# An attention kernel for short sequences: no pairing copy of q and k rows, transposes in column halves, two load buffers of each

## Chip, cores, metric

One core of one Trainium2 chip. The metric is the device time of one execution in microseconds (us), as a median over repeated runs, and as a ratio. Ratios are the mean time of one kernel's fast runs over that of the other's fast runs of the same rounds, so they are not quite the ratio of the medians that are quoted. A run is called slow when it is over 1.5% above the fastest of its kernel; verdicts use the fast ones. The profile is of one execution; its span is that of the program on the core, 1.8 us under the time of the same execution.

## The reference

```python
batch, n_heads, seq, head_dim = 32, 12, 128, 64        # q, k, v: f32, randn * 0.1
scores = matmul(q, k^T) / sqrt(64)
attn   = exp(scores - max); attn = attn / (sum(attn) + 1e-8)
out    = matmul(attn, v)
```

384 heads of 128 x 64. Every input and the output is 12.58 MB in f32.

## The kernel before

Units of 8 heads, 48 in all. A "super" is four units: one slab of q, one of k and one group of v, 1 MiB of f32 each, turned into bf16 by the load (the page has 512.0 KB landed per load). GpSimd (POOL) issues all 36 loads and 40 of the 48 stores, in one queue. A unit takes one step; in a step TensorE transposes a quarter of the q and k slabs of a later super (half of one slab in each step), puts the rows of one v unit in order, computes the scores of the next unit and the values of the present one. VectorE copies the transposes out of PSUM (the tiles that end in `_ps`) and normalises; ScalarE does exp and copies v.

The parts that matter here, cut (cuts are marked by `# ...`):

```python
NQ, NVB, NVE, NP, NT, NA = 4, 2, 8, 4, 2, 4        # four buffers of q and of k, two of v
PERIOD, FIRST = 8, -8
TRIPS = NU // PERIOD + 1                           # NU = 48 units, 7 trips

def transposes(t):                                 # TensorE, 8 to a step
    x = pair[t_index[t] % NP]
    # ...
    for r in range(8):
        i = nc.tensor.transpose(p[:, :, r4, jj, :], x[:, r].rearrange("p a d -> p (a d)"), ident[:])

def pair_up(t):                                    # VectorE: rows of two half slabs side by side
    src = (q_b, k_b)[j][s % NQ][:].rearrange("p a (r d) -> p r a d", d=D)
    return nc.vector.tensor_copy(pair[t_index[t] % NP][:], src[:, 8 * b:8 * b + 8])

def pool_load(kind, x):
    # v: waits until TensorE has ordered group x - 2; q and k: until slab x - NQ has been paired
    # ...

# TensorE alone runs a loop; the other engines' programs are straight.
with nc.Fori(0, TRIPS, engines=..., head_slot={nc.tensor.engine: 128}):
    for skipped, always, some in places:           # eight steps, each with T, V, S, O
        run_waits("PE", always)
        with nc.tensor.If_ne(trip, skipped):       # the first or the last trip skips this part
            for o, w in some:
                run("PE", o, w)
```

Two things in this loop will matter. The program holds eight steps of code, and the first trip begins at step -8, of which three steps are empty: it jumps over their code, and over scores and values that are not due yet. And `head_slot` sets the place in TensorE's code at which the loop begins, here 128; runs below move it.

The softmax here doesn't subtract the row's maximum and nothing guards it: scores larger than these inputs give would overflow.

Of the kernel before, what the change touches and what calls it, by code (L numbers as in the profile page):

```python
# [10 lines left out]
def kernel(  # L11
# [7 lines left out]
    nc = tc.nc  # L19
    f32 = mybir.dt.float32  # L20
    bf16 = mybir.dt.bfloat16
    EXP = mybir.ActivationFunctionType.Exp

    B, H, S, D = q.shape
# [7 lines left out]
    NU = B * H // 8  # L32
# [25 lines left out]
    vgroups = [4] * (NU // 4)  # L58
# [13 lines left out]
    t_at, v_at = {}, {}  # L72
    for s, (R, f) in enumerate(supers):
        J = R // 4
        for x in range(J):
            j, b = divmod(x, J // 2)
            t_at.setdefault(f - J - 1 + x, []).append((s, j, b))
    for m in range(NU):
        v_at[m - 3] = [m]
    steps = range(min(t_at) - 2, NU + 1)  # L80

    NQ, NVB, NVE, NP, NT, NA = 4, 2, 8, 4, 2, 4



    MIXED, OWN, HELD = 24, 40, NU - 8
# [3 lines left out]
    def sb(name, shape, dtype):  # L90
        return ctx.enter_context(nc.sbuf_tensor(name, shape, dtype))
# [5 lines left out]
    ident = sb("ident", [128, 128], bf16)  # L97
    sel = {R: sb(f"sel{R}", [128, 8, 2, 32], bf16) for R in (16,)}
    q_b = [sb(f"q_b{i}", [128, 2, 16 * D], bf16) for i in range(NQ)]
    k_b = [sb(f"k_b{i}", [128, 2, 16 * D], bf16) for i in range(NQ)]  # L100
    v_b = [sb(f"v_b{i}", [128, 4, RV * D], bf16) for i in range(NVB)]
    v_e = [sb(f"v_e{i}", [128, 8, D + 1], bf16) for i in range(NVE)]
    pair = [sb(f"pair{i}", [128, 8, 2, D], bf16) for i in range(NP)]
    qkT = [sb(f"qkT{i}", [128, 2, 16, S], bf16) for i in range(NT)]
    attnT = [sb(f"attnT{i}", [128, 2, 4, S], bf16) for i in range(NA)]
    o_sb = [sb(f"o_sb{c}", [128, n * 2 * RO * D], f32) for c, n in enumerate(stores)]
# [16 lines left out]
    program = {e: [] for e in ("PE", "ACT", "DVE", "POOL", "SP")}  # L123
# [5 lines left out]
    def op(engine, key, emit, deps=(), marks=(), dma=()):  # L129
        o = Op()  # L130
        o.key, o.emit, o.deps, o.marks, o.dma = key, emit, deps, marks, dma
        assert key not in position, key
        position[key], engine_of[key] = len(program[engine]), engine
        program[engine].append(o)
# [34 lines left out]
    def transposes(t):  # L169

        s, j, b = t
        R = supers[s][0]
        x = pair[t_index[t] % NP]
        p = qk_ps[:].rearrange("p (h r j s) -> p h r j s", h=R, r=4, j=2)
        for r in range(8):
            jj, r4 = divmod(r, 4)
            i = nc.tensor.transpose(  # L177
                p[:, :, r4, jj, :], x[:, r].rearrange("p a d -> p (a d)"), ident[:])
        return i

    def order_v(m):
# [61 lines left out]
            in_=s_ps[u % 2][:].rearrange("p a (h r j s) -> p (a h r) s j", h=4, r=4, j=J),  # L243
            func=EXP, bias=0.0, scale=scale)

    def pair_up(t):

        s, j, b = t
        src = (q_b, k_b)[j][s % NQ][:].rearrange("p a (r d) -> p r a d", d=D)
        return nc.vector.tensor_copy(pair[t_index[t] % NP][:], src[:, 8 * b:8 * b + 8])  # L250

    def keep_qk(t):
        s, j, b = t
        R = supers[s][0]
        J = R // 4
        x = qkT[s % NT][:, j, :R, :]
        if J == 2:
            return nc.vector.tensor_copy(x.rearrange("p h x -> p (h x)"), qk_ps[:])
        return nc.vector.tensor_copy(  # L259
            x.rearrange("p h (r j s) -> p (h r) j s", r=4, j=J)[:, :, 2 * b:2 * b + 2, :].rearrange(  # L260
                "p x j s -> p x (j s)"),
            qk_ps[:].rearrange("p (x y) -> p x y", x=R * 4))
# [15 lines left out]
    t_order = [t for u in steps for t in t_at.get(u, [])]  # L278
    t_index = {t: i for i, t in enumerate(t_order)}
    t_step = {t: u for u in steps for t in t_at.get(u, [])}  # L280
    vstep_of = {m: u for u in v_at for m in v_at[u]}
    s_q = [tc.alloc_semaphore(f"s_q{i}") for i in range(NQ)]
    s_k = [tc.alloc_semaphore(f"s_k{i}") for i in range(NQ)]
# [7 lines left out]

    def pe_transposes(t):
        i = t_index[t]
        deps = [("P", t)] + ([("E", t_order[i - 1])] if i else [])
        op("PE", ("T", t), lambda: transposes(t), deps, ["pe_dve"])

    def pe_wait(kind, key):
        op("PE", (kind, None), None, [key])
# [18 lines left out]
    def v_landing(m):  # L317
        if m == NU or vplace[m][1]:
            return []
        g = vplace[m][0]  # L320
        return [(s_v[g % NVB], 16 * (g // NVB + 1))]
# [8 lines left out]
        deps = [("S", u)] + ([("Q", u - NA)] if u >= NA else [])  # L330
        op("ACT", ("X", u), lambda: exps(u), deps, ["act_pe"])

    def dve_pair(t):
        s, j, b = t
        deps = [("T", t_order[t_index[t] - NP])] if t_index[t] >= NP else []
        dma = [((s_q, s_k)[j][s % NQ], 16 * (s // NQ + 1))]
        op("DVE", ("P", t), lambda: pair_up(t), deps, ["dve_io"] if t_index[t] else ["dve_pe", "dve_io"], dma)

    def dve_keep(t):
        s = t[0]  # L340
        deps = [("T", t)]
        for x in range(s):
            if x % NT == s % NT:
                R, f = supers[x]
                deps.append(("S", f + R // 4 - 1))
        op("DVE", ("E", t), lambda: keep_qk(t), deps, ["dve_pe"])

    def dve_normalise(u):
        c, w, n, first = splace[u]
# [10 lines left out]
    def pieces(c):  # L360

        first = sum(stores[:c])
        return 2 if 1 < stores[c] < supers[of_unit[first]][0] // 4 else 1

    own = [c for c in range(len(stores)) if sum(stores[:c + 1]) <= OWN]

    def lane(c):

        return c % 4 + (4 if c in own else 0)

    def store(c):
        name = "POOL" if c in own else "SP"
        e = ENGINE[name]
        n = stores[c]
        first = sum(stores[:c])
        R, f = supers[of_unit[first]]
        J = R // 4

        def emit():
            dst = o_rows[:, 2 * f:2 * f + 2 * J, :].rearrange("p (a w) e -> p a w e", a=2)[  # L380
                :, :, first - f:first - f + n, :]
            src = o_sb[c][:].rearrange("p (a w e) -> p a w e", a=2, w=n)
            if pieces(c) == 1:
                e.dma_start(out=dst, in_=src).then_inc(s_o[lane(c)], 16)  # L384
            else:
                for a in range(2):
                    e.dma_start(out=dst[:, a], in_=src[:, a]).then_inc(s_o[lane(c)], 16)  # L387

        last = first + n - 1
        op(name, ("store", c), emit, [("N", last if c in own else max(last, HELD))])  # L390

    def pool_load(kind, x):
        deps = []
        if kind == "v":
            if x >= NVB:
                deps = [("V", sum(vgroups[:x - NVB + 1]) - 1)]
            n, first = vgroups[x], sum(vgroups[:x])
            op("POOL", ("load", kind, x), lambda: nc.gpsimd.dma_start(  # L398
                out=v_b[x % NVB][:, :n, :], in_=v_rows[:, first:first + n, :],
            ).then_inc(s_v[x % NVB], 16), deps)  # L400
            return
        R, f = supers[x]
        j = "qk".index(kind)
        rows, bufs, sm = ((q_rows, q_b, s_q), (k_rows, k_b, s_k))[j]
        if x >= NQ:
            deps = [("P", t) for t in t_order if t[0] == x - NQ and t[1] == j]
        n = f * 8 // R

        def emit():
            nc.gpsimd.dma_start(  # L410
                out=bufs[x % NQ][:], in_=rows[R][:, n:n + 2, :]).then_inc(sm[x % NQ], 16)

        op("POOL", ("load", kind, x), emit, deps)


    op("ACT", ("K", -1), lambda: nc.scalar.drain(), [], ["act_pe"], v_landing(0))
    at_step = {}
    for u in steps:
        start = len(program["PE"])
        for t in t_at.get(u, []):  # L420
            pe_transposes(t)
        if u == t_step[t_order[-1]] + 1:
            pe_wait("T", ("E", t_order[-1]))
        for m in v_at.get(u, []):
            pe_order_v(m)
            act_keep(m)
        if u - 1 == vstep_of[NU - 1]:
            pe_wait("V", ("K", NU - 1))
        if 0 <= u + 1 < NU:
            pe_scores(u + 1)  # L430
            act_exps(u + 1)
        if 0 <= u < NU:
            pe_values(u)
        if 0 <= u - 1:
            dve_normalise(u - 1)
        elif u == 0:
            op("DVE", ("M", -1), None, [], ["dve_pe"])
            op("DVE", ("N", -1), lambda: nc.vector.drain(), [], ["dve_pe"])
        for t in t_at.get(u, []):
            dve_keep(t)  # L440
        for t in t_at.get(u + 2, []):
            dve_pair(t)
        for o in program["PE"][start:]:
            at_step[o.key] = u

    loads = []
    for s in range(len(supers)):
        for j in range(2):
            loads.append((t_step[s, j, 0] - 2, "qk"[j], s))
    for g in range(len(vgroups)):  # L450
        m = sum(vgroups[:g])

        loads.append((vstep_of[m] - 1.5 + (2 if 2 <= g < len(vgroups) - 2 else 0), "v", g))
    loads.sort(key=lambda e: e[0])
    todo = list(range(len(stores)))
    for _, kind, x in loads:
# [3 lines left out]
    for c in todo:  # L460
        store(c)

    c = counts()
    seen = {e: {} for e in program}
    waited_dma = {e: {} for e in program}

    def waits_of(engine, o):
        out = []
# [133 lines left out]
```

## Time and profile before

| | before |
|---|---|
| time, median of 4 runs | 132.18 us (131.85 to 133.28) |
| span of the profiled run, which took 133.72 us | 131.9 us |
| read and written in HBM | 37.75 and 12.58 MB |
| TensorE, VectorE, ScalarE busy | 74, 69, 56% |
| last v group landed | 113.70 us |

The prediction below shows the lines for the bound (transfers), the gap in them and a step on the engines. What it leaves out are the groups that the change touches. Columns: line, engine, operation, output from inputs, shapes, count; then total busy time and mean of one in ns; then idle time of the engine before them.

```profile
L177 PE MATMUL qk_ps<-ident,pair 128*128 128x128 bf16 x384 | 32.2, 232 | 15.3 <-PEq L478 15.1
...
L177 PEld LDWEIGHTS qk_ps<-ident,pair 128*128 128x128 bf16 x384 | 24.2, 103 | 20.4 <-issue 17.9
...
L250 DVE COPY pair<-q_b 128x1024 bf16<-128x1024 bf16 x24 | 11.1, 460 | 6.3 <-DMA q_b<-in_q_dram 6.2
L250 DVE COPY pair<-k_b 128x1024 bf16<-128x1024 bf16 x24 | 10.2, 427 | 0.0
```

Eight transposes of 128 columns to a step, 384 in all, each with one load of 128 stationary columns (128x128 in the LDWEIGHTS row), and 48 pairing copies of 0.44 us on VectorE. One more part of the page also belongs here, and I passed over it: the table of DMA queues (packets, MB, share of the 16 engines' time).

```profile
q0 software_dynamic: 16064, 29.36, 101.3%
q1 hardware_dynamic: 2176, 2.10, 4.7%
q8 instruction: 4, 0.07, 0.2%
```

Queue 8 carries four packets, 0.07 MB, and the table calls its content instructions. That they are TensorE's I take from the experiments: in a_first5 TensorE goes on 2.3 to 2.4 us after the start of each of three such packets.

One thing about this profile was passed over as well: its execution took 133.72 us, longer than any of the four timed ones and 1.5 us over their median. It counts as fast, but it is not a typical run.

### The profile page before, as it was taken

The page shows a single profiled execution, that of the slowest core. Times are in us where ns is not written, and L with a number is a line of the kernel's source. Part 1 is how long each engine was busy: PE and PEld are TensorE (multiplying, and loading weights), DVE is VectorE, ACT ScalarE, POOL GpSimd, SP SyncE. Part 2 cuts the span into 40 slices and gives each one's busy share as a digit, 9 for nine tenths or more (in the row PEclk, how much of TensorE's full clock was granted, in tenths as well). Part 3 has the DMA queues.
Part 4 walks back from the last instruction along what each step waited for, and adds up shares of the span by engine and source line. Part 5 has one row for each costly group of instructions (what it writes and reads, how often), then busy time and mean ns, then how long its engine had stood idle before and what let it go on. Part 6 is the DMA issues. An engine that isn't in the chain of part 4 may idle for free. (4 is left out here: it accounts for less than half of the span.)

```text
span 131.9 us, 7079 instructions
## 1 busy us (share of the span) xinstructions
PE 97.0 (74%) x3072; PEld 68.9 (52%) x3072; DVE 90.8 (69%) x214; ACT 73.7 (56%) x97; POOL 55.5 (42%) x81
## 2 busy tenths in 40 slices
PE   0014989994989999869849839978669998877610
PEld 0013647672667677656627626656456766555410
DVE  1126366895588999969939848969826988875740
ACT  0000528845577778476367366498084868588700
POOL 5950005015008259194460391390680399930000
PEclk9999999999599999999999999999986999999955
DMA  2999999999999999999999999999999999999982
GB/s 15 164 206 210 208 208 213 209 207 212 204 213 165 167 222 237 209 327 251 208 318 259 209 279 217 212 353 220 212 348 225 211 342 270 400 380 368 319 289 82
DMA packets 18248, 31.56 MB, mean 239 GB/s; under 512 B 1344, under 2 KB 9536, under 8 KB 18240
## 3 DMA queue, kind: packets, MB, share of 16 engines
q0 software_dynamic: 16064, 29.36, 101.3%
q1 hardware_dynamic: 2176, 2.10, 4.7%
q8 instruction: 4, 0.07, 0.2%
q14 instruction: 4, 0.03, 0.1%
HBM read 37.75 MB, written 12.58 MB: 381 GB/s over the span
## 5 line engine op out<-in xcount | busy, mean ns | idle before, releaser
L241 ACT ACTIVATE attnT<-s_ps 128x1024 bf16<-128x1024 f32 x48 | 49.4, 1030 | 0.4 <-PE s_ps L217 0.4
L236 ACT CAST v_e<-v_ps 128x512 bf16<-128x512 f32 x48 | 28.2, 588 | 37.0 <-PE v_ps L191 19.1
L177 PE MATMUL qk_ps<-ident,pair 128*128 128x128 bf16 x384 | 32.2, 232 | 15.3 <-PEq L478 15.1
L191 PE MATMUL v_ps<-v_b,sel 128*32 128x256 bf16 x768 | 31.9, 289 | 11.3 <-PEq L478 11.2
L272 DVE TENSOR_TENSOR o_sb<-o_ps,recip 128x512 f32<-128x512 f32 (+1 forms) x53 | 34.0, 641 | 4.8
L259 DVE COPY qkT<-qk_ps 128x1024 bf16<-128x1024 bf16 x48 | 32.8, 684 | 5.3 <-PE qk_ps L177 4.3
L177 PEld LDWEIGHTS qk_ps<-ident,pair 128*128 128x128 bf16 x384 | 24.2, 103 | 20.4 <-issue 17.9
L398 POOL DMA_DIRECT2D v_b<-in_v_dram x12 | 9.5, 791 | 59.7 <-PE v_ps L191 59.7
L387 POOL DMA_DIRECT2D out_dram<-o_sb x38 | 27.2, 729 | 0.0
L191 PEld LDWEIGHTS v_ps<-v_b,sel 128*32 128x32 bf16 x768 | 16.9, 99 | 17.8 <-issue 13.6
L228 PE MATMUL o_ps<-v_e,attnT 128*32 128x65 bf16 x1536 | 22.6, 200 | 1.7 <-PEq L478 0.8
L269 DVE RECIPROCAL recip<-o_ps 128x8 f32<-128x8 f32 (+1 forms) x53 | 10.5, 198 | 16.8 <-PE o_ps L228 16.0
L228 PEld LDWEIGHTS o_ps<-v_e,attnT 128*32 128x32 bf16 x1536 | 16.7, 98 | 7.5 <-issue 3.8
L217 PE MATMUL s_ps<-qkT 64*128 64x128 bf16 x384 | 19.5, 222 | 0.7 <-PEq L478 0.6
L217 PEld LDWEIGHTS s_ps<-qkT 64*128 64x128 bf16 x384 | 11.1, 95 | 11.3 <-issue 11.3
L250 DVE COPY pair<-q_b 128x1024 bf16<-128x1024 bf16 x24 | 11.1, 460 | 6.3 <-DMA q_b<-in_q_dram 6.2
L250 DVE COPY pair<-k_b 128x1024 bf16<-128x1024 bf16 x24 | 10.2, 427 | 0.0
L410 POOL DMA_DIRECT2D q_b<-in_q_dram x12 | 9.0, 747 | 1.0 <-SPq L96 1.0
L236 ACT ACT_TABLE_LOAD x1 | 1.3, 1283 | 13.7 <-DMA v_b<-in_v_dram 13.7
L410 POOL DMA_DIRECT2D k_b<-in_k_dram x12 | 8.6, 721 | 0.0
L560 DVE COPY sel<-ident 128x128 bf16<-128x128 bf16 x2 | 0.4, 224 | 1.8 <-POOL ident L537 1.8
L384 POOL DMA_DIRECT2D out_dram<-o_sb x2 | 1.5, 734 | 0.0
(8 smaller groups left out, 1.4 us busy)
## 6 DMA issues: line engine op xcount, KB each, us to landing
out_dram<-o_sb POOLq DMA_DIRECT2D x40, 256.0 KB, 10.2
q_b<-in_q_dram POOLq DMA_DIRECT2D x12, 512.0 KB, 13.2
k_b<-in_k_dram POOLq DMA_DIRECT2D x12, 512.0 KB, 12.7
v_b<-in_v_dram POOLq DMA_DIRECT2D x12, 512.0 KB, 10.2
out_dram<-o_sb SPq DMA_DIRECT2D x8, 256.0 KB, 4.3
```

Source lines behind the costliest of these rows:

```text
L177: i = nc.tensor.transpose(p[:, :, r4, jj, :], x[:, r].rearrange("p a d -> p (a d)"), ident[:])
L191: x = nc.tensor.matmul(t[r4 * 32:(r4 + 1) * 32, i, :, :], lhsT=pick[:, w * nh + i, jv, :], rhs=v_b[g % NVB][:, :n, (4 * jv + r4) * D:(4 * ...
L217: i = nc.tensor.matmul(t[:, a, h, :], lhsT=x[p, 1, 4 * w + h, :], rhs=x[p, 0, 4 * w + h, :], start=True, stop=True)
L228: y = nc.tensor.matmul(t[h * SO:(h + 1) * SO, a, r * (D + 1):(r + 1) * (D + 1)], lhsT=x[:, a, h, r * SO:(r + 1) * SO], rhs=v_e[m % NVE][:, ...
L236: return nc.scalar.copy(v_e[m % NVE][:, :, :D], v_ps[:].rearrange("p (n e) -> p n e", e=D))
L241: return nc.scalar.activation(out=attnT[u % NA][:].rearrange("p a h (r s j) -> p (a h r) s j", r=4, j=J), in_=s_ps[u % 2][:].rearrange("p ...
L250: return nc.vector.tensor_copy(pair[t_index[t] % NP][:], src[:, 8 * b:8 * b + 8])
L259: return nc.vector.tensor_copy(x.rearrange("p h (r j s) -> p (h r) j s", r=4, j=J)[:, :, 2 * b:2 * b + 2, :].rearrange("p x j s -> p x (j ...
L269: nc.vector.reciprocal(r, o4[:, :, :, D]).then_inc(s_r, 1)
L272: return nc.vector.tensor_mul(o[:, :, w, :].rearrange("p a (r d) -> p a r d", d=D), o4[:, :, :, :D], r.unsqueeze(3).to_broadcast([128, o4. ...
L387: e.dma_start(out=dst[:, a], in_=src[:, a]).then_inc(s_o[lane(c)], 16)
L410: nc.gpsimd.dma_start(out=bufs[x % NQ][:], in_=rows[R][:, n:n + 2, :]).then_inc(sm[x % NQ], 16)
```

## The change

The intent: the pairing copy only brings two rows of 64 together so that one transpose fills 128 columns. TensorE can take either row from the landed tile and write it to its own half of the PSUM partitions (the changed kernel's page has 768 such transposes, with loads of 128x64), so VectorE loses 48 copies, and with the copies gone the number of q and k buffers falls from four to two (the loop's code names the buffers, and eight steps hold two supers). The core of the diff:

```diff
-    NQ, NVB, NVE, NP, NT, NA = 4, 2, 8, 4, 2, 4
+    NQ, NVB, NVE, NT, NA = 2, 2, 8, 2, 4
@@ transposes
-        x = pair[t_index[t] % NP]
+        x = (q_b, k_b)[j][s % NQ][:].rearrange("p a (r d) -> p r a d", d=D)[:, 8 * b:8 * b + 8]
         for r in range(8):
             jj, r4 = divmod(r, 4)
-            i = nc.tensor.transpose(
-                p[:, :, r4, jj, :], x[:, r].rearrange("p a d -> p (a d)"), ident[:])
+            for a in range(2):
+                i = nc.tensor.transpose(
+                    p[a * D:(a + 1) * D, :, r4, jj, :], x[:, r, a], ident[:])
@@ the landing of the next slab is now waited for ahead of the copy out of PSUM
-        op("DVE", ("E", t), lambda: keep_qk(t), deps, ["dve_pe"])
+        op("DVE", ("E", t), lambda: keep_qk(t), deps, ["dve_pe"], qk_landing(t_index[t] + 1))
@@ pool_load
-            deps = [("P", t) for t in t_order if t[0] == x - NQ and t[1] == j]
+            deps = [("T", t) for t in t_order if t[0] == x - NQ and t[1] == j]
@@ order of the loads
-            loads.append((t_step[s, j, 0] - 2, "qk"[j], s))
+            loads.append((t_step[s, j, 0], "qk"[j], s))
-        loads.append((vstep_of[m] - 1.5 + (2 if 2 <= g < len(vgroups) - 2 else 0), "v", g))
+        loads.append((vstep_of[m] + 0.5, "v", g))
```

Left out: the removal of `pair` and `pair_up`, and that stores wait for a matmul of the next unit in place of VectorE's mark.

## The prediction

> **What bounds the kernel now.** I read the page first, then the waits, then stretches of the timeline, then the completions of the DMAs that the trace records. The page's first lines:
>
> ```profile
> span 131.9 us, 7079 instructions
> PE 97.0 (74%) x3072; PEld 68.9 (52%) x3072; DVE 90.8 (69%) x214; ACT 73.7 (56%) x97; POOL 55.5 (42%) x81
> ...
> DMA  2999999999999999999999999999999999999982
> GB/s 15 164 206 210 208 208 213 209 207 212 204 213 165 167 222 237 209 327 251 208 318 259 209 279 217 212 353 220 212 348 225 211 342 270 400 380 368 319 289 82
> ...
> HBM read 37.75 MB, written 12.58 MB: 381 GB/s over the span
> ```
>
> No compute engine passes 74%, while the DMA row is full from the second slice to the end. The GB/s row counts what lands: loads turn f32 into bf16, so 208 landed means 416 read. Stores alone land at 350 to 400. The whole is thus a queue of transfers, and the completions in the trace give its pace: in a full queue one load (1 MiB read) finishes every 2.50 us, one store (256 KB) every 0.625 us. 36 loads and 48 stores make 90 + 30 = 120 us; the first load, issued at 1.5, lands at 8.6, so the transfer itself cannot start before about 6.1. What remains of the 131.9 us is a few us of gaps and a tail. Where are the gaps? The page shows 165 and 167 in the 13th and 14th slices. Windows of 1 us (columns: us, busy of PE, PEld, DVE, ACT, POOL, clock, DMA share, GB/s):
>
> ```profile
> 40.00:41.00 1.00, 1.00 (x48) 0.81 (x44) 0.66 (x3) 1.00 (x2) 0.77 (x2) 1.00 1.11 209
> 41.00:42.00 1.00, 1.00 (x28) 0.59 (x25) 0.99 (x2) 0.67 (x2) 1.00 (x2) 1.00 0.83 146
> 42.00:43.00 1.00, 1.00 (x48) 0.79 (x46) 0.90 (x4) 1.00 (x2) 1.00 (x2) 1.00 0.77 120
> ```
>
> The queue ran dry. The timeline of POOL, which issues all loads, says why:
>
> ```profile
> 30.75 0.73 POOL L410 DMA_DIRECT2D q_b<-in_q_dram  x1
> 40.23 0.74 POOL L398 DMA_DIRECT2D v_b<-in_v_dram  x1 [8.75 <-PE v_ps L191]
> ```
>
> From 31.5 to 40.2 nothing was issued: the load of v group 4 waits until TensorE has ordered v group 2, and the q and k loads stand behind it. By the completions, the q slab ahead of it landed at 43.61 and v group 4 at 47.14, 3.53 us later and not 2.50; the next k took 3.43. So 1.0 + 0.9 = 1.9 us of transfer were lost. A load issued into an empty queue takes about 6.9 us to land (7.1 for the first, 6.91 for this one), so it should have been issued by 39.2.
>
> The last v group lands at 113.70 (ScalarE starts on it at 113.78). Without any gap it would be 8.58 + 35 x 2.50 + 24 x 0.625 = 111.1, the 24 being the stores queued ahead of it. After it come units 44 to 47 and the last stores: 131.9 - 113.7 = 18.2 us. That tail is the second thing that sets the end.
>
> Last, a full-speed step (one of 48 units) on TensorE and VectorE, from the timeline:
>
> ```profile
> 61.16 0.61 PE L177 MATMUL qk_ps<-ident,pair 128*128 128x128 bf16 x8 [0.17 <-PEq L478]
> 61.41 0.69 DVE L272 TENSOR_TENSOR o_sb<-o_ps,recip 128x512 f32<-128x512 f32 x1
> ...
> 61.71 0.62 PE L191 MATMUL v_ps<-v_b,sel 128*32 128x256 bf16 x16
> 62.02 0.68 DVE L259 COPY qkT<-qk_ps 128x1024 bf16<-128x1024 bf16 x1
> 62.26 0.40 PE L217 MATMUL s_ps<-qkT 64*128 64x128 bf16 x8
> ...
> 62.59 0.31 PEld L228 LDWEIGHTS o_ps<-v_e,attnT 128*32 128x32 bf16 x32
> 62.59 0.43 PE L228 MATMUL o_ps<-v_e,attnT 128*32 128x65 bf16 x32
> 62.62 0.42 DVE L250 COPY pair<-k_b 128x1024 bf16<-128x1024 bf16 x1
> ...
> 63.01 0.61 PE L177 MATMUL qk_ps<-ident,pair 128*128 128x128 bf16 x8
> ```
>
> From start to start: transposes 0.55, v ordering 0.55, scores 0.33, values 0.42, together 1.85 us. VectorE needs 0.20 + 0.69 + 0.68 + 0.42 = 1.99 of overlapping durations in it, so both engines are full in such a step. Four steps take 7.4 us, and the three loads that feed them 7.5: while no stores are in the queue, compute and transfers run level. Once two to four stores ride with each three loads, a group costs 8.75 to 10 us of transfer and compute has slack.
>
> [...]the 32 value matmuls[...] span 0.43 us; less one duration of 0.20, that is 7.4 ns from one to the next[...]. [...]32 loads of 32 columns span 0.31 us, less 0.10 for one, 6.8 ns each[...], and they hide behind the matmuls. [...]No row here shows a 64-column load.[...]
>
> **The change part by part.**
> - Removed: 48 pairing copies on VectorE, 11.1 + 10.2 = 21.3 us of busy time. VectorE's step falls from 1.99 to 1.57. That is not on the path: TensorE's 1.85 stays, and the transfers bound most of the run. In the opening the first transposes no longer follow a copy: 9.35 becomes about 8.7, and some 0.6 us are gained per early step, but the q1 slab, landing at 16.14, gates the same point.
> - Added: 384 transposes become 768 of half width. Now (0.61 - 0.23) / 7 = 54 ns each. If the two halves run at once, eight pairs at 54 ns are again 0.43 us plus the turn-around of 0.12. [...]I take +0.00 to +0.05 us a step.
> - Moved: the landing of the next slab is now waited for ahead of the copy out of PSUM, which is in order on VectorE as the pairing was: the same coupling, one slab ahead. Stores wait for a matmul of the next unit instead of VectorE's mark: under a step later, on stores that are long ready.
> - Buffers: six loads go out at once and not nine. From then on q(s+2) waits for the transposes of q(s), k(s+2) for those of k(s), v for the ordering as before. By hand, with the durations above (cold transposes and orderings at 1.03, as the timeline has them until 19 us): q2 is issued at 11.7, k2 at 15.9, v2 at 20.7, q3 at 21.4, v3 at 28.4, v4 at 36.0. In a full queue these would land at 23.6, 26.1, 28.6, 31.1, 36.1 and 43.6, so v2, v3 and v4 must be issued by 21.7, 29.2 and 36.7. All hold, with 1.0, 0.8 and 0.7 us to spare. The order matters: v2 is now the ninth load and not the tenth, so TensorE is not left waiting for it (1.89 us idle before 32.10 now, followed by transposes and orderings at 1.03 until 36 at a lower granted clock, which is what made v4 late).
>
> Sum: the 1.9 us gap goes, nothing else on the path changes. The tail has transposes in two of its seven steps and no pairing that ends last. 132.25 - 1.9 = 130.3; I add 0.4 for small new gaps at such thin margins: **130.7 us**.
>
> **Rivals.** (a) The halves run one after another[...]: +0.43 us per step, 2.28. A group of four is then 9.1 us against 7.5 of transfer, and v2 to v5 come late by about 0.3 + 3 x 1.6 + 0.4 = 5.5 us, which replaces the 1.9: about 136. Against it stand the values rows; for it, that no row shows transposes in column halves. (b) The third buffers were needed: a gap as now appears elsewhere early, and the gain is nil: 132 to 133. For it: margins below 1 us. Against it: in both kernels v's two buffers hold back the whole POOL queue already. (c) All is hidden and the relief of VectorE also shortens the tail: all of the 2.6 us of lateness of the last v and some of the tail vanish, 129. Against it: the tail's end is the chain values, reciprocal, multiply with one PSUM buffer, untouched.
>
> **Range and chances.** (a) about 12%, (b) about 25%, the main line 45%, (c) 18%. Range 128.8 to 134.0. Over 2% faster needs less than 129.6: 0.18. Within 2%: 0.70. Slower: 0.12.
>
> **What would show it.** Transposes 16 to a step in about 0.6 us of busy time, 32 us in all, and a step of 1.85 to 1.9 (rival a: 50 us and 2.3). VectorE's busy time near 70 us. No slice of 165 GB/s between 40 and 48 us, and the last v group landing near 111.5 with about 18 us after it. Wrong would be: a lower GB/s in slices 7 to 14, POOL waiting long for transposes with an emptying queue, or a tail over 19 us.

## The result, and the profile after

139.16 us median (136.87 to 140.07, 4 runs) against 132.18: ratio 1.041 (95% interval 1.029 to 1.054). The change made the kernel 4% slower; 130.7 was predicted, with 134.0 as the upper end. Two of the four runs count as slow; the ratio is of the other two, 136.87 and 138.74. The profiled run of the changed kernel is its fastest, 136.87.

Its page, the lines that answer to those shown of before:

```profile
span 135.1 us, 7822 instructions
...
PE 97.0 (72%) x3456; PEld 69.8 (52%) x3456; DVE 75.3 (56%) x166; ACT 73.7 (55%) x97; POOL 55.0 (41%) x81
...
DMA  1999999499999999999999999999999999999990
GB/s 13 178 204 210 208 211 204 86 195 206 166 191 147 177 213 283 211 244 326 211 244 325 212 246 247 213 317 252 210 321 250 211 323 275 397 397 368 343 302 14
...
q8 instruction: 5, 0.08, 0.2%
...
HBM read 37.75 MB, written 12.58 MB: 373 GB/s over the span
```

The engines have not become the bound: TensorE's 97.0 us are the same as before to the last digit. But the DMA row has a hole in its eighth slice (digit 4), where GB/s falls to 86, and the slices around the 13th are still low, so the hole that the change was to close has moved forward and grown. The transposes themselves:

```profile
L177 PE MATMUL qk_ps<-ident,q_b 128*64 128x128 bf16 x384 | 16.6, 232 | 12.6 <-PEq L472 12.6
...
L177 PEld LDWEIGHTS qk_ps<-ident,q_b 128*64 128x64 bf16 x384 | 13.0, 116 | 15.3 <-issue 14.5
...
L177 PE MATMUL qk_ps<-ident,k_b 128*64 128x128 bf16 x384 | 16.6, 232 | 4.0 <-PEq L472 4.0
```

768 now, 16.6 + 16.6 = 33.2 us busy against 32.2. Sixteen half-width ones to a step span 0.64 us where eight took 0.61. So a step's transposes take 0.03 us longer, inside the +0.00 to +0.05 of the prediction.

Where does the hole come from? First the three windows around it (us, busy of PE, PEld, DVE, ACT, POOL, clock, DMA share, GB/s), then POOL's issues:

```profile
23.00:24.00 1.00, 1.00 (x35) 0.69 (x29) 0.67 (x1) 0.10 (x1) 0.00 (x0) 1.00 1.11 213
24.00:25.00 1.00, 1.00 (x56) 0.81 (x48) 0.29 (x3) 1.00 (x2) 0.83 (x2) 1.00 0.24 45
25.00:26.00 1.00, 1.00 (x35) 0.59 (x30) 1.00 (x2) 0.64 (x2) 0.60 (x1) 1.00 0.10 15
```

```profile
17.95 0.71 POOL L407 DMA_DIRECT2D k_b<-in_k_dram  x1 [6.76 <-PE qk_ps L177]
24.16 0.74 POOL L395 DMA_DIRECT2D v_b<-in_v_dram  x1 [5.51 <-PE v_ps L191]
24.89 0.70 POOL L407 DMA_DIRECT2D q_b<-in_q_dram  x1
```

v group 2 is issued at 24.16. The prediction's hand schedule had it at 20.7 and said that it must be out by 21.7. It waited 5.51 us for TensorE. And TensorE, with VectorE's copies that it depends on:

```profile
12.51 0.69 DVE L253 COPY qkT<-qk_ps 128x1024 bf16<-128x1024 bf16 x1 [1.25 <-PE qk_ps L177]
...
13.06 1.04 PE L191 MATMUL v_ps<-v_b,sel 128*32 128x256 bf16 x16 [0.59 <-PEq L472]
16.59 1.07 PE L177 MATMUL qk_ps<-ident,k_b 128*64 128x128 bf16 x16 [2.48 <-PEq L472]
17.58 1.04 PE L191 MATMUL v_ps<-v_b,sel 128*32 128x256 bf16 x16
...
19.66 0.69 DVE L253 COPY qkT<-qk_ps 128x1024 bf16<-128x1024 bf16 x1 [1.28 <-PE qk_ps L177]
...
20.53 0.41 PE L217 MATMUL s_ps<-qkT 64*128 64x128 bf16 x8
...
22.66 0.64 PE L177 MATMUL qk_ps<-ident,q_b 128*64 128x128 bf16 x16 [1.73 <-PEq L472]
23.23 0.62 PE L191 MATMUL v_ps<-v_b,sel 128*32 128x256 bf16 x16
```

This is the place to stop at. The transposes at 16.59 wait for one thing only, VectorE's copy of the transposes before them, which ended at 12.51 + 0.69 = 13.20; the ordering before them ended at 14.10. The profile writes "PEq" for what ended the idle time (2.48 us here), and no other engine or DMA. The same at 22.66: the copy ended at 20.35, the scores at 20.94. TensorE stood for 2.48 and 1.73 us with all its semaphores met. In the old kernel the fourth and the sixth transposes follow without a stop:

```profile
15.06 1.03 PE L177 MATMUL qk_ps<-ident,pair 128*128 128x128 bf16 x8
...
19.72 0.62 PE L177 MATMUL qk_ps<-ident,pair 128*128 128x128 bf16 x8
```

The changed kernel's two stops are together 4.2 us, and v group 2 is 3.5 us late by the schedule.

### The profile page after: what moved, and what is told of

Its sections match the earlier page's. It is cut to its first block, busy times and chain, and to the rows that moved or that the text cites. A ratio compares the mean times of both kernels' runs of the same rounds, so it can differ in the third digit from the quotient of the medians.

```text
span 135.1 us, 7822 instructions
## 1 busy us (share of the span) xinstructions
PE 97.0 (72%) x3456; PEld 69.8 (52%) x3456; DVE 75.3 (56%) x166; ACT 73.7 (55%) x97; POOL 55.0 (41%) x81
## 2 busy tenths in 40 slices
DMA packets 18249, 31.58 MB, mean 234 GB/s; under 512 B 1344, under 2 KB 9536, under 8 KB 18240
## 5 line engine op out<-in xcount | busy, mean ns | idle before, releaser
L177 PE MATMUL qk_ps<-ident,q_b 128*64 128x128 bf16 x384 | 16.6, 232 | 12.6 <-PEq L472 12.6
L228 PE MATMUL o_ps<-v_e,attnT 128*32 128x65 bf16 x1536 | 21.8, 197 | 1.8 <-PEq L472 0.9
L177 PEld LDWEIGHTS qk_ps<-ident,q_b 128*64 128x64 bf16 x384 | 13.0, 116 | 15.3 <-issue 14.5
L228 PEld LDWEIGHTS o_ps<-v_e,attnT 128*32 128x32 bf16 x1536 | 15.9, 97 | 7.3 <-issue 3.1
L177 PE MATMUL qk_ps<-ident,k_b 128*64 128x128 bf16 x384 | 16.6, 232 | 4.0 <-PEq L472 4.0
L395 POOL DMA_DIRECT2D v_b<-in_v_dram x12 | 9.0, 751 | 23.2 <-PE v_ps L191 23.2
L177 PEld LDWEIGHTS qk_ps<-ident,k_b 128*64 128x64 bf16 x384 | 13.0, 116 | 6.3 <-issue 4.7
## 6 DMA issues: line engine op xcount, KB each, us to landing
q_b<-in_q_dram POOLq DMA_DIRECT2D x12, 512.0 KB, 11.7
```

The source lines that it names most:

```text
L177: i = nc.tensor.transpose(p[a * D:(a + 1) * D, :, r4, jj, :], x[:, r, a], ident[:])
L228: y = nc.tensor.matmul(t[h * SO:(h + 1) * SO, a, r * (D + 1):(r + 1) * (D + 1)], lhsT=x[:, a, h, r * SO:(r + 1) * SO], rhs=v_e[m % NVE][:, ...
L395: op("POOL", ("load", kind, x), lambda: nc.gpsimd.dma_start(out=v_b[x % NVB][:, :n, :], in_=v_rows[:, first:first + n, :],).then_inc(s_v[x ...
```

## The experiments

After looking at the traces I had three theories. **Theory 1**: in those two gaps TensorE waits for its own instructions. The DMA records of the trace hold packets of 16 KB on queue 8, one after another, and the changed kernel has five where the old one has four:

```
start of each 16 KB packet on queue 8, us
before          2.56   8.19  14.86  20.45
changed         2.58   8.30  13.92  19.62  24.00
```

The gaps end 2.7 and 3.0 us after the start of the third and the fourth. The loop body grew by 64 transposes with their loads, 128 instructions. **Theory 2**: two buffers of q and k are too few in themselves. **Theory 3**: the column halves cost TensorE something on the path that the rows do not show.

Twelve kernels ran, in four calls; each call timed the kernel before beside its kernels, and the ratios are to that. By the rule of 2% the record calls a_same, a_head32 and a_head70 slower, b_nq2, b_dead1, a_wrong8 and a_konly the same, and the other five unclear; the intervals of those five all lie above 1.

### The first pass begun three steps later in the code (label a_first5)

```diff
-    PERIOD, FIRST = 8, -8
+    PERIOD, FIRST = 8, -5
```

> The changed kernel with the first pass of TensorE's loop begun three steps later in the code (FIRST -5 for -8): the same work in the same order, but the first pass no longer skips over code. Theory 1 (TensorE stood at 14.1 to 16.6 and 20.9 to 22.7 us for its own instructions, fetched 16 KB at a time through the full DMA engines): both stalls go, v2 is issued near 20.7 and not 24.2, no dry queue at 24 to 26 us, last v lands near 112, time 130 to 132. Theory 2 (two buffers of q and k are too few in themselves): nothing changes, 136 to 140. Theory 3 (the column-half transposes cost TensorE more than the rows show): nothing changes either.

141.48 us, ratio 1.068 (1.056 to 1.080): slower, not faster. As a forecast of theory 1 it failed, yet its trace is the best witness for it. TensorE now runs through the dense code of all eight steps in the first pass and stands in the middle of a group of matmuls, where no instruction waits for anything (v group 2 was issued at 22.98 and not near 20.7):

```profile
22.59 0.61 PE L217 MATMUL s_ps<-qkT 64*128 64x128 bf16 x8
23.14 0.57 PE L228 MATMUL o_ps<-v_e,attnT 128*32 128x65 bf16 x27
25.82 0.23 PE L228 MATMUL o_ps<-v_e,attnT 128*32 128x65 bf16 x5 [2.11 <-issue]
```

```profile
30.50 0.29 PE L228 MATMUL o_ps<-v_e,attnT 128*32 128x65 bf16 x6
32.08 0.47 PE L228 MATMUL o_ps<-v_e,attnT 128*32 128x65 bf16 x26 [1.29 <-issue]
32.97 0.64 PE L177 MATMUL qk_ps<-ident,q_b 128*64 128x128 bf16 x16 [0.41 <-PEq L472]
```

32 values matmuls of one step are one stretch of code without a wait; 27 of them run, 2.11 us pass, and the other five run. In the second fence six run, 1.29 us pass, 26 run. From the one stop to the other TensorE executes 5 + 16 + 16 + 8 + 32 + 16 + 16 + 8 + 6 = 123 matmuls with as many weight loads, 246 instructions; with the branches and waits in between, some ten by my estimate, that is about 256. Such a stretch is called a block below. From the stop before that, which ended at 19.75, to 25.82 it executes 91 and jumps over the 32 values matmuls of one step: 123 again. The packets on queue 8 start at 11.08, 17.42, 23.40 and 29.69, and a fifth at 89.55, beside which the trace shows no stop; TensorE resumes at 19.75, 25.82 and 32.08, each 2.3 to 2.4 us after one of them. From this I take it that TensorE stands for its instructions. What was wrong in my forecast was the premise that the packets come ahead of need: these four start 6.0 to 6.3 us apart, with one block of instructions run from one to the next, and a dense stretch uses up a block in about 3.3 us, an estimate from 1.85 us for the 144 instructions of a step.

### The kernel before with longer code (b_dead), its control (b_dead1), two buffers (b_nq2), and both (b_dead_nq2)

These four take the change apart without its transposes. Code that is never executed, at the head of the loop:

```diff
+        never = ctx.enter_context(nc.tensor.register("never"))
+        nc.tensor.reg_mov(never, 0)
         with nc.Fori(0, TRIPS, ...):
+            with nc.tensor.If_ne(never, 0):
+                for _ in range(64):          # b_dead1: range(1)
+                    nc.tensor.transpose(qk_ps[:, :128], pair[0][:, 0]..., ident[:])
```

Two buffers, with the loads in the changed kernel's order:

```diff
-    NQ, NVB, NVE, NP, NT, NA = 4, 2, 8, 4, 2, 4
+    NQ, NVB, NVE, NP, NT, NA = 2, 2, 8, 4, 2, 4
-            loads.append((t_step[s, j, 0] - 2, "qk"[j], s))
+            loads.append((t_step[s, j, 0], "qk"[j], s))
-        loads.append((vstep_of[m] - 1.5 + (2 if 2 <= g < len(vgroups) - 2 else 0), "v", g))
+        loads.append((vstep_of[m] + 0.5, "v", g))
```

b_dead:

> The kernel before with 64 transposes (128 instructions with their weight loads) at the head of TensorE's loop that a branch always jumps over: its code becomes as long as the changed kernel's, its work stays. Theory 1: the same kind of stalls of about 2 us each in the first pass (a fifth 16 KB fetch), but nine loads were issued ahead, so little of it reaches the end: 132 to 135. Theory 2 and 3: no stall, 132.

b_nq2:

> The kernel before with two buffers of q and of k and the changed kernel's order of loads; pairing stays. Theory 1: without the longer code the two buffers cost nothing, 130.5 to 133, v2 issued near 21. Theory 2: loads come late from then on, 135 to 139. Theory 3: 132.

b_dead_nq2:

> Both: the kernel before with the jumped-over code and with two buffers, transposes untouched. Theory 1: the stalls now meet a short queue, and the loss of the changed kernel is there without its transposes: 135 to 139, dry queue near 24 us. Theory 2: as b_nq2. Theory 3: 132 as before.

b_dead1, run later:

> Control for the jumped-over code: the kernel before with the same branch and register over one transpose and not 64. Theory 1: 132 to 133.5, ratio 0.995 to 1.01. If the branch itself cost the time and not the length of the code: 136.5 to 137.5.

| kernel before with | buffers | median, us | ratio (95%) | v group 2 issued, us |
|---|---|---|---|---|
| nothing (profile of the first run) | 4 | 132.2 | 1 | 21.20 |
| a branch over 1 transpose | 4 | 132.58 | 0.998 (0.994 to 1.001) | 19.99 (a slow run) |
| a branch over 64 transposes | 4 | 137.28 | 1.032 (1.023 to 1.042) | 25.30 |
| two buffers | 2 | 133.03 | 1.003 (1.000 to 1.007) | 20.19 |
| both | 2 | 139.05 | 1.048 (1.039 to 1.057) | 26.08 |
| the changed kernel | 2 | 139.16 | 1.041 (1.029 to 1.054) | 24.16 |

128 instructions that no execution ever reaches cost 3.2%, and the control says that it is their length and not the branch. Two buffers cost 0.3%: theory 2 falls as the cause of the 4%. Both together make the whole loss without a single half-width transpose, so theory 3 is not needed. The stops are where theory 1 wants them (here b_dead, which stands a third time, 2.55 us before its second transposes at 11.39), again with a fifth packet on queue 8:

```profile
16.96 1.01 PE L177 MATMUL qk_ps<-ident,pair 128*128 128x128 bf16 x8 [1.69 <-PEq L478]
...
23.26 0.75 PE L177 MATMUL qk_ps<-ident,pair 128*128 128x128 bf16 x8 [2.33 <-PEq L478]
```

I had expected b_dead at 132 to 135, because nine loads are out ahead in it. That was too low: the deeper queue takes back only about a third of the loss (1.032 against 1.048). In b_nq2, on the other hand, the order of issues is the changed kernel's, and v2 and q3 come out within 0.5 us of what the prediction had worked out by hand for that kernel (20.7, 21.4):

```profile
20.19 0.74 POOL L398 DMA_DIRECT2D v_b<-in_v_dram  x1 [7.35 <-PE v_ps L191]
20.92 0.70 POOL L410 DMA_DIRECT2D q_b<-in_q_dram  x1
21.61 0.72 POOL L410 DMA_DIRECT2D k_b<-in_k_dram  x1
```

### The same instructions at another place (a_same, a_head64, a_head32, b_head224)

If the blocks matter, moving the loop within a block must change the time, though not one instruction differs. Where the expectations place blocks and boundaries, they are estimates from the count of 246 and some ten.

```diff
-                head_slot={nc.tensor.engine: 128}):
+                head_slot={nc.tensor.engine: 64}):      # a_head32: 32; the kernel before, b_head224: 224
```

a_same:

> The changed kernel once more, for the comparison on this chip: 136.5 to 140, stalls of TensorE near 14 to 16.6 and 21 to 22.7 us.

a_head64:

> The changed kernel, its loop laid at slot 64 of a block of 256 instructions and not at 128; not one instruction differs. From the places where TensorE stood in the run begun later (all 246 counted instructions apart, some 10 branches and waits between them), the body is about 1206 instructions and now ends before a block boundary, with the boundary ahead of it one step later. Theory 1 (fetches of instruction blocks in the first pass): the stall at 14.1 us goes to the next step and shrinks to about 1.6 us, that at the loop's end goes; v2 issued near 20.5, time 130.5 to 133.5. Theory 2 and 3 (buffers, transposes): 137 to 140 as before.

a_head32:

> As a_head64 with slot 32: the loop's end is still inside the fourth block, but a boundary falls between the second and the third transposes. Theory 1: 130.5 to 134.5 if that block is there in time, one stall of about 2 us at 9 to 12 us otherwise. Theory 2 and 3: 137 to 140.

b_head224:

> The kernel before, its loop laid at slot 224: the block boundaries fall as in the changed kernel, one ahead of the fourth transposes and one before the loop's end; no instruction differs. Theory 1: it loses what the jumped-over code lost, 135.5 to 138, with stalls near 14 and 21 us. Theory 2 and 3: 132.

Medians and ratios: a_same 139.10 (1.044, 1.034 to 1.054; a second profile of the changed kernel, with stops of 2.22 and 2.20 us and v group 2 issued at 25.46), a_head64 136.79 (1.026, 1.018 to 1.034), a_head32 139.58 (1.044, 1.033 to 1.054; its profiled run was a slow one), b_head224 136.44 (1.024, 1.012 to 1.035). b_head224 is as expected: the old kernel, moved by 96 slots, loses 2.4% and has stops of 2.62 and 1.68 us before its transposes at 17.21 and 23.36, and one of 0.93 us inside its second transposes. a_head64 gained half of what I expected and a_head32 nothing. Both traces say why: a_head64 fetches twice before its first transposes (packets at 2.32 and 2.86), which then begin at 8.25 and not 7.2 us, and it stands again inside an ordering of v; a_head32 stops after 14 of its first 16 transposes (2.10 us) and again for 3.96 us before the third set.

### Slot 70 (a_head70)

```diff
-                head_slot={nc.tensor.engine: 128}):
+                head_slot={nc.tensor.engine: 70}):
```

> The changed kernel, correct, loop at slot 70: as slot 64, but the place where the first pass jumps in no longer straddles a boundary (slot 64 paid two fetches before its first transposes, which began at 8.25 and not 7.2). Theory 1: first transposes at 7.2, one stall of about 1 us in the ordering of v1, v2 issued near 20.5, 131.5 to 133.5 (ratio 0.99 to 1.01). Theory 3 (column halves cost something of their own): 137 to 140.

143.82 us, ratio 1.080 (1.068 to 1.091), the slowest of all. Three of its five runs count as slow (the fast ones took 141.52 and 142.28), and so does the profiled one (span 147.2), so only the form of its trace is used here. The first pass went as expected (transposes at 7.31, one stop of 0.92 us inside an ordering, v group 2 issued at 21.33). But in the second pass TensorE stood again:

```profile
16.50 0.62 PE L191 MATMUL v_ps<-v_b,sel 128*32 128x256 bf16 x8 [0.92 <-issue]
...
21.69 0.64 PE L177 MATMUL qk_ps<-ident,k_b 128*64 128x128 bf16 x16
25.66 0.62 PE L191 MATMUL v_ps<-v_b,sel 128*32 128x256 bf16 x16 [3.33 <-issue]
...
29.42 0.58 PE L228 MATMUL o_ps<-v_e,attnT 128*32 128x65 bf16 x28
31.83 0.21 PE L228 MATMUL o_ps<-v_e,attnT 128*32 128x65 bf16 x4 [1.83 <-issue]
```

Queue 8 has nine packets, at 23.28, 29.53, 33.87, 42.43 and 46.94 us after the four of the first pass: five more, as many as the changed kernel has in all. Why this slot has packets in the second pass and the others do not, no run shows. What is shown is that the same instructions take 1.026, 1.044, 1.044 or 1.080 of the old kernel's time (slots 64, 128, 32 and 70, fast runs) by their place alone.

### The rest of the change with short code (a_wrong8, a_konly)

a_wrong8 gives a wrong result on purpose: one transpose of 128 columns as they lie in the landed tile, so that the code is as short as before, without pairing and with two buffers.

```diff
-            for a in range(2):
-                i = nc.tensor.transpose(
-                    p[a * D:(a + 1) * D, :, r4, jj, :], x[:, r, a], ident[:])
+            y = (q_b, k_b)[j][s % NQ][:, r // 4, (8*b + 2*(r % 4))*D:(8*b + 2*(r % 4) + 2)*D]
+            i = nc.tensor.transpose(p[:, :, r4, jj, :], y, ident[:])
```

> Wrong result on purpose: the changed kernel with 8 transposes to a step of 128 columns as they lie in the landed tile (two rows of one slab), so TensorE's code is as short as before; no pairing, two buffers, waits as in the changed kernel. Theory 1: 130.5 to 133, v2 issued near 20.5, one stall of some 1.6 us before the fifth transposes. Theory 2 (buffers, moved waits): 136 to 140. Theory 3 (column halves themselves): 130.5 to 133 too, so this run separates only 1 and 3 from 2.

133.25 us, ratio 1.003 (1.000 to 1.006), v group 2 issued at 21.54, four packets on queue 8. (The comparison with the reference lets it pass: with inputs scaled by 0.1 the scores are so small that attention is nearly uniform. It still computes other scores.) So the two buffers, the missing pairing and the moved waits together cost nothing that the times show; the halves themselves are not in this run. Its profile (133.48 us) is not without a hole: GB/s falls to 154 and 180 in the eighth and ninth slices, and v group 2, though issued inside the prediction's 21.7, landed 7.96 us later, 4.07 after the load ahead.

a_konly is by its construction correct: column halves for k alone, q rows paired as before, two buffers. The body grows by 64 instructions and not by 128.

```diff
+            if j == 0:
+                i = nc.tensor.transpose(p[:, :, r4, jj, :], pair[(2*s + b) % 4][:, r]..., ident[:])
+                continue
             for a in range(2):
                 i = nc.tensor.transpose(p[a * D:(a + 1) * D, :, r4, jj, :], x[:, r, a], ident[:])
```

> Correct result: two buffers and the changed kernel's waits, column halves for the k rows alone, q rows paired on VectorE as before. TensorE's loop body is then about 1142 instructions, so that at slot 128 it ends before the boundary that the changed kernel's crosses, and the fourth transposes come before the boundary ahead of them. Theory 1: one stall of 1 to 1.6 us near 15 to 17 us, none at the loop's end, v2 issued near 21, no fifth fetch, ratio 0.99 to 1.015 (131.5 to 134). Theory 3 (column halves cost something of their own on the path): half of the changed kernel's loss, ratio about 1.02, 135 to 136.

134.16 us, ratio 1.006 (1.002 to 1.009), v group 2 issued at 20.18, one stop of 0.60 us inside an ordering. Half of the half-width transposes at about an eighth of the loss, by fast runs. But 10 of its 20 runs count as slow, against 4 of 25 of the old kernel, and by the medians of all runs it is 1.2% behind. Its profiled run is a fast one:

```profile
span 130.8 us, 7451 instructions
...
GB/s 14 167 199 206 212 207 211 205 212 204 209 212 203 206 273 216 193 349 225 211 343 232 211 282 217 220 348 216 215 352 221 211 352 271 404 397 368 315 316 30
...
q8 instruction: 4, 0.07, 0.2%
```

Four packets again, and a GB/s row without a hole until the end.

The packets of five of these, with the issue of v group 2:

```
                starts of 16 KB packets on queue 8, us                          v 2 issued
changed         2.58   8.30  13.92  19.62  24.00                                24.16
b_dead          2.68   8.70  14.29  19.94  25.64                                25.30
b_nq2           2.57   8.43  13.88  19.41                                       20.19
a_wrong8        2.57   8.16  13.73  19.28                                       21.54
a_konly         2.58   8.09  13.67  19.86                                       20.18
```

No version beats the kernel before. b_nq2 and a_wrong8 come within 0.3% of it with half the q and k buffers, a_konly within 0.6%.

## Why the prediction was wrong

Point by point, by its own steps.

- **Bound and queue of transfers: right.** Loads still land 2.5 us apart when the queue is full (2.49, from 67.09 to 69.58). In the changed kernel v groups 2, 3 and 4 and q slab 4 landed 4.19, 4.59, 3.50 and 2.94 us after the load ahead of them and not 2.50: 1.7 + 2.1 + 1.0 + 0.4 = 5.2 us lost, where the old kernel's gap cost 1.9. The difference of 3.3 is about that of the profiled spans (135.1 - 131.9 = 3.2). The last v group landed at 116.18 us; 111.5 was predicted. The tail after it is 135.1 - 116.18 = 18.9 us, inside the 19 that the prediction set as a limit.
- **Pairing copies: right in kind.** VectorE fell from 90.8 to 75.3 us, 15.5 and not 21.3 (records of VectorE overlap: the groups on the page add up to 99.0 us for 90.8 before, 77.9 for 75.3 after), off the path as said: two buffers cost 1.003 with the copies (b_nq2) and 1.003 without (a_wrong8).
- **Column halves: right.** 33.2 us busy for 32 predicted, a step of 1.87 us (61.38 to 63.25) for 1.85 to 1.9. The matmuls follow each other 27 ns apart, (0.64 - 0.23) / 15, 54 for a pair. 16 loads of 64 columns span 0.51 us; less one of 0.12 that is 26 ns from one to the next, 52 for a pair. That the two halves would run at once was my assumption: for it the prediction has only 32-column matmuls, 7.4 ns apart, and says itself that no row shows transposes in column halves.
- **"q2 is issued at 11.7, k2 at 15.9, v2 at 20.7 ... v4 at 36.0": this step failed.** They came at 10.49, 17.95, 24.16 and 39.68. I had worked the schedule from durations and semaphores, and took for granted that TensorE always has its next instruction. The term that was missing is the fetch of a longer loop body: a stop of 2.48 us before the fourth transposes and one of 1.73 us at the loop's end. The issue times themselves were sound: b_nq2 and a_konly, whose shorter code shows no stop at these two places (and one of 0.60 us elsewhere in a_konly), issue v2 at 20.19 and 20.18, and b_nq2 v3 and v4 at 28.44 and 36.29.
- **"+0.00 to +0.05 us a step" for the added transposes** was right per step and wrong per run. Their cost is not in the time of execution but in 128 more instructions, paid once, in the first pass, when the queue had 0.7 to 1.0 us to spare by the prediction's schedule: after the packet at 24.00 us queue 8 of the changed kernel carries nothing to the end.
- **The margins of 1.0, 0.8 and 0.7 us** I had called thin, and they were: a delay of 3.5 us emptied the queue, and since four steps of compute (7.4 us) and the three loads that feed them (7.5) run level until stores come in, loads went on landing late up to v group 4, at 48.29. The 6.9 us from issue to landing, on which the margins rest, was not a constant: v2 took 5.75 in the changed kernel and 7.96 in a_wrong8.
- **Rivals.** (a) fell by the rows. (b), the buffers, fell by b_nq2 as a cause of the loss, and the short queue only adds to a delay once there is one (1.048 against 1.032); but its forecast, a gain of nil, is what the versions with short code give. The true cause was none of the three. What pointed to it stood on the page, as the "instruction" row of the queue table, and in the listing of the program's order, where eight transposes a step become sixteen inside a loop.
- **"132.25 - 1.9 = 130.3": this step failed too.** The gap of 1.9 us was read in an execution that took 133.72 us and taken off a median of 132.25. In b_nq2's profile the gap is gone (no slice under 198 GB/s from the third to the last but one; the last completion of v group 4 still came 3.50 us after that of the load ahead, but the DMA share stays above 1.0 from 36 to 50 us, so no transfer stood still) and that execution took 132.44, 1.3 us less than the old kernel's profiled one; but over 20 and 23 timed runs the medians are 133.03 against 132.96. So the gain, where it showed, was over an untypical run. The one other profile of nearly the old kernel, b_dead1, has the gap too (v group 4 landed 4.45 us after the load ahead), in a run that counts as slow (134.35). Whether the usual executions have it stays open, as none was profiled.
- **"Cannot start before about 6.1 us"** was misread. A load ends with sixteen completion marks (1344 in either trace for 84 loads and stores). In the old kernel's profile fifteen of the first slab's came by 6.73 us and the last at 8.58; in b_nq2 and the changed kernel the last came at 6.84 and 6.83. The load queue's packets began at 3.0 us in all three. So one part of sixteen lagged by 1.9 us: last completions, by which the losses here and above are counted, can overstate or hide a loss. And the first transposes of the changed kernel began at 7.19 and not at 8.7.

What stays open besides: what decides when a packet of instructions starts. The packets follow each other 5.4 to 6.7 us apart while the loads fill the DMA engines (DMA share 1.16 from 12 to 19 us in both kernels), and the stops end 2.3 to 3.3 us after a packet starts; in the changed kernel the fifth, at 24.00, came 4.4 us after the fourth, while the queue was dry (share 0.24 from 24 to 25 us). No run here shows what sets these times.

Open too is why the transposes and orderings up to 19 us, which the prediction calls cold, took 1.01 to 1.04 us: from 12 to 19 us the old kernel's granted clock was 1.00, as it was when the same work took 0.62 (19 to 28 us). At the lower clock of which the prediction speaks, 0.50 from 33 to 36 us, they took 1.03 and 1.04.

## What to carry to other kernels

Count instructions, not only their time: here the first pass of a loop on TensorE stood for 2.48 and 1.73 us, until 2.7 and 3.0 us after the start of an instruction packet, while the loads ran, and 128 more instructions cost 3.2% without being executed, though a step's sixteen small transposes took only 0.03 us more than its eight. When an engine stands with its semaphores met, above all inside a group that waits for nothing, look at the instruction packets in the DMA records and at where the loop begins (1.026 to 1.080 here, by the slot alone). And where the start of a kernel decides when its buffers come free, test a change of code length alone, with instructions that are jumped over, before blaming the work or the buffers. And before taking a gap in a profile off the median time, see what the profiled execution itself took.
